# More rooms for the weight halves in the three double gate blocks of a fused decoder block

## The chip, the cores and the metric

The kernel runs on one core of one Trainium2 chip. The time is the device time of one execution in microseconds (us), taken as the median of the runs. The reader meets five engines and a queue: PE (TensorE, the matrix products), DVE (VectorE), ACT (ScalarE), POOL (GpSimd) and SP (SyncE), whose queue issues nearly all loads from memory. PEld is the part of PE that loads the stationary operand of a product.

## The reference

One layer of a decoder: 256 rows of 2048 numbers in float32. The input is normalised and modulated (shift, scale and gate come from a vector c through `w_ada`), and one wide projection `w_in` feeds three token mixers (stick-breaking attention, dilated attention, gated linear attention) and the gates of the three branches. What matters here are these lines:

```python
proj = h @ w_in
... gate_cols = the last 3 * 2048 columns of proj
g = jax.nn.sigmoid(gate_cols.reshape(b, t, N_BRANCH, d))
y = g[:, :, 0] * (o_sb @ w_br_sb) + g[:, :, 1] * (o_dil @ w_br_dil) + g[:, :, 2] * (o_gla @ w_br_gla)
x = x + gate1 * (y @ w_out)
```

After it comes a feed-forward part of the same kind (`w_ffn_in`, `w_ffn_out`). The gate columns are cut into four blocks of 512 columns for each of the three branches: twelve blocks of 2048 x 512 weights, times the 256 x 2048 matrix h.

## The kernel before

**Products.** Every float32 weight is split into two halves, hi (the weight rounded to the matrix engine's format) and lo (the rest), and each product is three matrix instructions: hi by hi, lo by hi, hi by lo (`mm3`, L173 to L175). The columns of h are the stationary operand, 128 x 512 weights the moving one, and the results add up in PSUM banks of 128 x 512.

**A weight tile's way.** A tile of 256 x 512 weights (512 KB) is loaded into a raw tile by SP (`raw_at`, L216), ACT copies it to the hi half (`split`, L236), DVE subtracts to give the lo half (`sub`, L222), and PE uses both. A place for a raw tile is called a raw here, a place for a pair of halves a room. The pool `wp` has four raws and four rooms; further ones are borrowed from named tiles of 128 x 1024 numbers or more that are out of use at the time, such as `T3`, `X1`, `X2`, `A9`, `A10`. `S(tag, ...)` takes the named tile; its new user waits until the last user of the old contents is done.

**Double blocks.** Of the twelve gate blocks, block 0 of each branch and block 3 of each are computed one by one (`gate_block`), and blocks 1 and 2 of a branch together (`gate_pair`, one call for each branch: 0, 1 and 2). `gate_pair` goes through eight steps, n = 0 to 7, in the order of `GATE_PAIRS`. Six steps are plain: two weight tiles (c0 and c1, one of each block), two rooms, 24 matrix instructions. Two of them (n = 2 and n = 5) are fast: two weight tiles r0 and r1 are combined by four more DVE subtractions, with `A0` and `A1` as places for the sums, to seven products instead of eight (Strassen's way), so that four rooms and 21 matrix instructions do. After the second fast step, the shared products are added to the results by `fast_products` (copy L315, sums L316 to L319, adds to the banks L273), the first two adds between steps 6 and 7, the others after step 7. A sigmoid (ACT, L1208) then writes the gates to `A7`/`X0` (branch 0), `A8`/`X1` (branch 1) and `T0`/`X2` (branch 2).

**Which raw and which room.** Both are taken in turn. With e extra rooms, room number i of a cycle of 4 + e is extra room i if i < e, else the next room of the pool. `gate_pair` sets the count so that each call begins with the four rooms of the pool. A call uses 20 rooms, numbered k = 0 to 19: k = 0, 1 in step 0; 2, 3 in step 1; 4 to 7 in step 2 (fast); 8 to 11 in steps 3 and 4; 12 to 15 in step 5 (fast); 16, 17 in step 6; 18, 19 in step 7. The raws, 16 in a call and numbered j = 0 to 15 (two in each step), go by a count that runs on from one call to the next.

**Order.** The weights of three steps are asked for ahead (`LOOK` = 3), with a raised priority (`prio`); the merging sums have twice that. The order of instructions on each engine is laid out beforehand by a planner, which takes the instruction of the highest priority that is ready by its own estimate of times; on the chip each engine keeps that order, and so does the SP queue with its loads. Between the splits lie the background sums for the modulation (`ada_mac`, L424), which read tiles of `w_ada` (L520) from a small ring; in the three double blocks they make the sum for gate1 in `T4` and `T5`. `ada` is the accumulator of the other background sums, 128 x 2048 numbers wide.

Of the kernel before, what the change touches and what calls it, by code (L numbers as in the profile page):

```python
# [11 lines left out]
F32R = mybir.dt.float32r  # L12
# [5 lines left out]
P = 128  # L18
# [5 lines left out]
NB = 512  # L24
# [56 lines left out]
def trunk(ctx: ExitStack, tc: tile.TileContext, I, out):  # L81
# [12 lines left out]
    def nm(base):  # L94
        uid[0] += 1
        return f"{base}_{uid[0]}"

    def S(tag, shape, dtype=F32):
        return slot.tile(shape, dtype, tag=tag, name=nm(tag))
# [13 lines left out]
    @contextmanager  # L113
    def prio(offset=AHEAD):

        with tc.high_priority(offset=offset):
            start = tc.cur_priority
            yield
            n = tc.cur_priority - start
        tc.cur_priority += n  # L120
# [80 lines left out]
    def sums_of(sf, h, a, b):  # L201

        (a0, b0), (a1, b1) = ((x[:, a, :], x[:, b, :]) for x in h)
        for dst, x, y, op in (
            (0, a1, b1, ALU.add), (2, a0, a1, ALU.subtract), (1, sf[:, 0], a0, ALU.subtract), (3, b0, sf[:, 1], ALU.subtract)
        ):
            nc.vector.tensor_tensor(sf[:, dst], x, y, op=op)

    def load_pair(src, p, c0, c1, fast, tags):


        def raw_at(c):
            more_raws = state.get("more_raws", ())
            i = state["raws"] = (state.get("raws", -1) + 1) % (4 + len(more_raws))
            raw = S(more_raws[i], [P, 2, NB]) if i < len(more_raws) else wp.tile([P, 2, NB], F32, tag="raw", name=nm("raw"))
            nc.sync.dma_start(raw, src[2 * p * P : (2 * p + 2) * P, c : c + NB].rearrange("(k p) c -> p k c", p=P))  # L216
            return raw

        def sub(dst, x, y):
            chain = state.get("chain")  # L220
            with tc.issue_after(chain.ins) if chain is not None else nullcontext():
                done = nc.vector.tensor_tensor(dst, x, y, op=ALU.subtract)  # L222
            if "chain" in state:
                state["chain"] = done
            return done

        def split(src):
            n = src.shape[1]
            more_rooms = state.get("more_rooms", ())
            i = state["tiles"] = (state.get("tiles", -1) + 1) % (4 + len(more_rooms))  # L230
            if i < len(more_rooms):
                hi, lo = (S(tag, [P, 2, NB], F32R) for tag in more_rooms[i])
            else:
                hi = wp.tile([P, 2, NB], F32R, tag="whi", name=nm("whi"), bufs=4)
                lo = wp.tile([P, 2, NB], F32R, tag="wlo", name=nm("wlo"), bufs=4)
            nc.scalar.copy(hi[:, :n, :], src)  # L236
            state["split"] = sub(lo[:, :n, :], src, hi[:, :n, :].bitcast(F32))
            return [(hi[:, i, :], lo[:, i, :]) for i in range(n)]

        with prio():  # L240
            if not fast:
                return [split(raw_at(c0)), split(raw_at(c1))]
            r0, r1 = raw_at(c0), raw_at(c1)
            b11, b21 = split(r0)
            ta, tb = (S(tag, [P, 2, NB]) for tag in tags)
            sub(ta[:, 0], r1[:, 0], r0[:, 0])
            sub(ta[:, 1], r1[:, 1], r1[:, 0])
            (b22,) = split(r1[:, 1:2])
            sub(tb[:, 0], r1[:, 1], ta[:, 0])
            sub(tb[:, 1], r0[:, 1], tb[:, 0])  # L250
            t1, t3 = split(ta)
            t2, t4 = split(tb)
            return b11, b21, b22, t1, t3, t2, t4

    def fast_products(src, c0, c1, order, at, sums, own, other, tags, hooks={}, more=False, look=None):
# [4 lines left out]
        def load(n):  # L260
            while len(ws) < min(n, len(order)):
                ws.append(load_pair(src, order[len(ws)][0], c0, c1, order[len(ws)][1], tags))
                splits.append(state["split"])
# [935 lines left out]
    def gate_pair(br, own, other, rooms, raws=()):  # L1199
        state["more_rooms"], state["more_raws"] = rooms, raws  # L1200
        state["tiles"] = len(rooms) - 1
        c0 = COL_G + br * D + NB
        o = fast_products(w_in, c0, c0 + NB, GATE_PAIRS, h_at, h_sums, own, other, ("A0", "A1"), look=LOOK)
        with prio():
            for i in range(2):
                g = S(gtags[1 + i][br], [P, NT, NB])
                for t in range(NT):
                    nc.scalar.activation(g[:, t, :], o[i][t], AF.Sigmoid)  # L1208
                gates[1 + i, br] = g
# [38 lines left out]
    for j in range(2):  # L1248
        hi = S(gtag[0][j], [P, 4, T], F32R)
        lo = S(gtag[1][j], [P, 4, T], F32R)  # L1250
# [64 lines left out]
    h_sums = sums_of_h()  # L1315
    state["rate"] = RATE_PAIRS
    ring["tags"], ring["spare"] = ("AR0", "AR1", "KD"), 1
    gate_pair(0, acc_bank, misc_bank, (("X1", "X2"), ("A9", "A10")), ("T3",))
    gate_pair(1, misc_bank, acc_bank, (("A9", "A10"),), ("X2", "T3"))
    gate_pair(2, acc_bank, misc_bank, (("A9", "A10"),), ("T3",))  # L1320
    ring["tags"] = ("AR0", "AR1", "KC", "KD")
    ring["spare"] = 2
    state["rate"] = RATE_Y
# [164 lines left out]
    for i in range(NFF):  # L1488
# [30 lines left out]
        if ftags[2 * i] == ftags[2 * i + 1]:  # L1519
            hl = S(ftags[2 * i], [P, 2, 4, T], F32R)  # L1520
            hi, lo = hl[:, 0], hl[:, 1]
        else:
            hi, lo = (S(tag, [P, 4, T], F32R) for tag in ftags[2 * i : 2 * i + 2])
# [140 lines left out]
```

## Time and profile before

| what | value |
|---|---|
| median of 3 runs (lowest to highest) | 1577.41 us (1577.26 to 1579.7) |
| the profiled execution | 1576.77 us, span 1575.0 us |
| PE busy | 1563.4 us, 99% of the span |
| DVE busy | 1394.3 us, 89% |
| ACT busy | 876.9 us, 56% |
| memory traffic | 255 GB/s over the span |

The span runs from the first to the last instruction of the profiled execution. A timeline row gives the start in us from the start of the span, the duration, the engine, the line, the operation, what it writes and reads (by tile names without numbers, so that `A` stands for any of A0 to A12, `X` for X0 to X2, `T` for T0 to T6), the shapes, and in square brackets the idle time before it with what ended that. The durations of matrix instructions overlap: the next one starts before the one before it ends, so the distance of two starts is what one costs. A row of waits gives the waiting instruction, what released it, the total in us, the number of times and the longest.

### The profile page before, as it was taken

The numbers are of one execution on the slowest core, as the hardware profiler recorded it, in microseconds if no ns is written. First come the engines' busy times: TensorE is split into PE (matmuls) and PEld (weight loads), VectorE is DVE, ScalarE is ACT, GpSimd is POOL, SyncE is SP. The second block draws the span as 40 slices with busy tenths as digits, with TensorE's granted clock in tenths as the row PEclk, the third lists the DMA queues.
The fourth block names the chain that finished last, engine by engine and source line by source line (L and its number), as shares of the span: only waits on it lengthen the run. The fifth ranks groups of instructions, "written<-read, shape, count | busy, mean of one in ns | idle before, by whom it ended". The sixth has DMA issues, their size and how long they took to land.

```text
span 1575.0 us, 20266 instructions
## 1 busy us (share of the span) xinstructions
PE 1563.4 (99%) x7186; PEld 1293.5 (82%) x7186; DVE 1394.3 (89%) x1704; ACT 876.9 (56%) x1215; POOL 12.6 (1%) x24
## 2 busy tenths in 40 slices
PE   8999999999999999999999999999999999999998
PEld 7878888888888788888888888888888888888887
DVE  6889996888888899987977888999999999899896
ACT  5654448875765545444435645556555555455553
POOL 1000000000000000000000000000000000000000
PEclk9999999999999999999999999999999999999999
DMA  9999997677787888989998886665666566876764
GB/s 333 361 326 323 336 308 239 221 237 224 240 293 256 269 290 273 316 255 320 305 329 258 299 301 205 188 212 188 201 203 211 174 201 231 291 229 202 222 212 136
DMA packets 196317, 402.26 MB, mean 255 GB/s; under 512 B 13102, under 2 KB 28116, under 8 KB 196216
## 3 DMA queue, kind: packets, MB, share of 16 engines
q1 hardware_dynamic: 194952, 397.75, 76.5%
q0 software_dynamic: 1088, 3.16, 0.5%
q8 instruction: 56, 0.92, 0.2%
q14 instruction: 45, 0.37, 0.1%
q10 hardware_dynamic: 176, 0.07, 0.0%
HBM read 395.68 MB, written 5.24 MB: 255 GB/s over the span
## 4 chain that ended last, share of the span: by engine, by line
PE 91%; DVE 4%; DMA 2%; ACT 2%; issue 1%; SPq 0%; DVEq 0%; ACTq 0%
PE acc L175 21%; PE acc L174 21%; PE acc L173 21%; PE misc L174 7%; PE misc L175 7%; PE misc L173 7%; DVE wlo L222 1%; PE acc L579 1%; PE misc L948 1%; DVE A L222 1%; PE misc L1287 1%; DVE T L424 0%; DVE wlo L166 0%; DMA A<-x 0%; PE misc L572 0%
## 5 line engine op out<-in xcount | busy, mean ns | idle before, releaser
L165 ACT CAST whi<-raw 128x1024 fp32r<-128x1024 f32 (+1 forms) x277 | 278.8, 1012 | 286.5 <-PE acc L175 193.1
L166 DVE TENSOR_TENSOR wlo<-raw,whi 128x1024 fp32r<-128x1024 f32 (+1 forms) x277 | 322.0, 1171 | 93.8 <-ACT whi L165 92.5
L173 PE MATMUL acc<-whi,H 128*128 128x512 f32 x997 | 390.5, 392 | 1.2 <-ACT H L591 0.8
L174 PE MATMUL acc<-wlo,H 128*128 128x512 f32 x997 | 388.9, 390 | 0.8 <-DVE wlo L166 0.7
L175 PE MATMUL acc<-whi,H 128*128 128x512 f32 x997 | 388.8, 391 | 0.5 <-DVE H L598 0.4
L175 PEld LDWEIGHTS acc<-whi,H 128*128 128x128 f32 x997 | 187.0, 188 | 40.2 <-DVE H L598 1.4
L173 PEld LDWEIGHTS acc<-whi,H 128*128 128x128 f32 x997 | 187.2, 188 | 39.9 <-ACT H L591 1.3
L174 PEld LDWEIGHTS acc<-wlo,H 128*128 128x128 f32 x997 | 187.4, 188 | 39.2 <-DVE wlo L166 1.7
L236 ACT CAST whi<-raw 128x1024 fp32r<-128x1024 f32 (+1 forms) x130 | 125.4, 975 | 66.0 <-PE acc L175 32.7
L222 DVE TENSOR_TENSOR wlo<-raw,whi 128x1024 fp32r<-128x1024 f32 (+1 forms) x130 | 144.1, 1125 | 15.9 <-ACT whi L236 14.9
L175 PE MATMUL acc<-whi,A 128*128 128x512 f32 x221 | 86.1, 389 | 0.0
L173 PE MATMUL acc<-whi,A 128*128 128x512 f32 x210 | 82.0, 390 | 0.0
L174 PE MATMUL acc<-wlo,A 128*128 128x512 f32 x210 | 81.7, 389 | 0.0
L174 PE MATMUL misc<-wlo,H 128*128 128x512 f32 (+1 forms) x190 | 73.6, 387 | 1.3 <-DVE wlo L222 1.3
L173 PE MATMUL misc<-whi,H 128*128 128x512 f32 (+1 forms) x190 | 73.6, 387 | 0.0
L175 PE MATMUL misc<-whi,H 128*128 128x512 f32 (+1 forms) x190 | 73.5, 387 | 0.0
L222 DVE TENSOR_TENSOR A<-raw,A 128x1024 fp32r<-128x1024 f32 (+2 forms) x54 | 53.8, 1002 | 1.3 <-ACT A L236 0.8
L424 DVE SCALAR_TENSOR_TENSOR ada<-AR,csil,ada 128x1024 f32<-128x1024 f32 x39 | 49.7, 1279 | 5.1 <-DMA AR<-w_ada 5.0
L175 PEld LDWEIGHTS acc<-whi,A 128*128 128x128 f32 x221 | 41.5, 188 | 8.7
L236 ACT CAST A<-raw 128x1024 fp32r<-128x1024 f32 (+1 forms) x36 | 35.9, 1003 | 21.7 <-PE acc L175 7.2
L174 PEld LDWEIGHTS acc<-wlo,A 128*128 128x128 f32 x210 | 39.4, 188 | 8.1
L173 PEld LDWEIGHTS acc<-whi,A 128*128 128x128 f32 x210 | 39.4, 188 | 8.0
(682 smaller groups left out, 3038.3 us busy)
## 6 DMA issues: line engine op xcount, KB each, us to landing
raw<-w_in SPq DMA_DIRECT2D x192, 512.0 KB, 4.7
raw<-w_ffn_in SPq DMA_DIRECT2D x135, 512.0 KB, 4.7
raw<-w_ffn_out SPq DMA_DIRECT2D x73, 512.0 KB, 4.7
AR<-w_ada SPq DMA_DIRECT2D x62, 512.0 KB, 4.9
raw<-w_out SPq DMA_DIRECT2D x32, 512.0 KB, 5.6
OS<-w_ada SPq DMA_DIRECT2D x24, 512.0 KB, 6.1
KD<-w_ada SPq DMA_DIRECT2D x22, 512.0 KB, 5.5
AR<-w_ffn_in SPq DMA_DIRECT2D x22, 512.0 KB, 4.2
```

The lines of the kernel that those rows point to most:

```text
L165: state["cast"] = nc.scalar.copy(hi[:, :n, :], raw[:, :n, :])
L166: state["split"] = nc.vector.tensor_tensor(lo[:, :n, :], raw[:, :n, :], hi[:, :n, :].bitcast(F32), op=ALU.subtract)
L173: nc.tensor.matmul(ps, lh, rh, start=start, stop=False, skip_group_check=seeded)
L174: nc.tensor.matmul(ps, lh, rl, start=False, stop=False, skip_group_check=seeded)
L175: state["mm"] = nc.tensor.matmul(ps, ll, rh, start=False, stop=stop, skip_group_check=seeded)
L222: done = nc.vector.tensor_tensor(dst, x, y, op=ALU.subtract)
L236: nc.scalar.copy(hi[:, :n, :], src)
L424: nc.vector.scalar_tensor_tensor(acc, raw, c, acc, op0=ALU.mult, op1=ALU.add)
L579: state["warm"] = nc.tensor.matmul(ps, ones_r, wide, start=True, stop=True)
L948: nc.tensor.matmul(ps[:n, t * N_GLA + h, :].rearrange("p (s l) -> p s l", l=L), at(f, h, t)[:, :n], odd(at(f, h, t)), start=True, stop=True,)
L1287: nc.tensor.transpose(ps[:, i, :], src[:, i * P : (i + 1) * P], ident)
```

## The change

The extra rooms and raws of the three calls are extended by named tiles. A room may now be one tile that holds both halves (`ada`). No load, no product and no sum is added or removed.

```diff
+    def room(tags):
+        if len(tags) == 1:
+            hl = S(tags[0], [P, 2, 2, NB], F32R)
+            return hl[:, 0], hl[:, 1]
+        return (S(tag, [P, 2, NB], F32R) for tag in tags)
...
             if i < len(more_rooms):
-                hi, lo = (S(tag, [P, 2, NB], F32R) for tag in more_rooms[i])
+                hi, lo = room(more_rooms[i])
...
-    gate_pair(0, acc_bank, misc_bank, (("X1", "X2"), ("A9", "A10")), ("T3",))
-    gate_pair(1, misc_bank, acc_bank, (("A9", "A10"),), ("X2", "T3"))
-    gate_pair(2, acc_bank, misc_bank, (("A9", "A10"),), ("T3",))
+    gate_pair(0, acc_bank, misc_bank, (("X1", "X2"), ("A9", "A10"), ("ada",)), ("T3", "T0", "A8"))
+    gate_pair(1, misc_bank, acc_bank, (("A9", "A10"), ("X1", "T0"), ("ada",)), ("X2", "T3"))
+    gate_pair(2, acc_bank, misc_bank, (("A9", "A10"), ("ada",)), ("T3", "T0"))
```

| call | rooms before, after | raws before, after |
|---|---|---|
| branch 0 | 6, 7 | 5, 7 |
| branch 1 | 5, 7 | 6, 6 |
| branch 2 | 5, 6 | 5, 6 |

## The prediction

> **What bounds the kernel now.** I read the page first, then who waits for whom on PE, then the busy time in the stretches of the three double blocks, and there the timeline.
>
> ```profile
> span 1575.0 us, 20266 instructions
> ...
> PE 1563.4 (99%) x7186; PEld 1293.5 (82%) x7186; DVE 1394.3 (89%) x1704; ACT 876.9 (56%) x1215; POOL 12.6 (1%) x24
> ```
>
> PE is busy all the time but 11.6 us, so no change that leaves the products as they are can bring more than that, and this one only the share that lies in the double blocks. Who waits on PE (the longest, 2.5, is the start of the kernel):
>
> ```profile
> PE misc L351 <- DMA H<-c: 2.5, 1, 2.5
> ...
> PE misc L174 <- DVE wlo L222: 1.3, 1, 1.3
> ...
> PE acc L173 <- DVE acc L273: 0.3, 1, 0.3
> ```
>
> ```profile
> core 0: us, PE busy (x) PEld busy (x) DVE busy (x) ACT busy (x) POOL busy (x), PEclk, DMA share, GB/s
> ...
> 490.90:533.80 42.90, 42.55 (x189) 34.92 (x187) 40.26 (x49) 22.24 (x30) 0.00 (x0) 1.00 0.86 284
> 533.80:577.60 43.80, 42.52 (x187) 34.84 (x186) 40.87 (x45) 24.58 (x29) 0.00 (x0) 1.00 0.82 269
> 577.60:619.80 42.20, 42.20 (x188) 34.95 (x187) 40.47 (x44) 22.36 (x25) 0.00 (x0) 1.00 0.82 269
> ```
>
> These are the three calls. PE has two holes in them, one in branch 0 and one in branch 1; branch 2 has none. DVE is busy 93 to 96% of each. The two holes by their starts:
>
> ```profile
> 527.51 0.39 PE L175 MATMUL acc<-A,H 128*128 128x512 f32 x1
> 528.25 0.47 PE L173 MATMUL acc<-whi,H 128*128 128x512 f32 x1 [0.34 <-DVE acc L273]
> ...
> 549.25 0.39 PE L175 MATMUL misc<-whi,H 128*128 128x512 f32 x1
> 549.48 0.40 PE L173 MATMUL misc<-whi,H 128*128 128x512 f32 x1
> 551.16 0.50 PE L174 MATMUL misc<-wlo,H 128*128 128x512 f32 x1 [1.28 <-DVE wlo L222]
> ```
>
> A matrix instruction costs 0.227 (branch 2: 186 of them, 6 x 24 + 2 x 21, in 42.2 us). So the holes cost 528.25 - 527.51 - 0.23 = 0.51 and 551.16 - 549.48 - 0.23 = 1.45: 1.96 us is all there is to win here.
>
> **Hole one (1.45, branch 1, step 3).** The lo half that PE waits for:
>
> ```profile
> 541.10 0.68 DVE L222 TENSOR_TENSOR A<-X,A 128x512 f32<-128x512 f32 x1
> ...
> 546.25 0.69 DVE L222 TENSOR_TENSOR A<-X 128x512 f32<-128x512 f32 x1 [1.54 <-DMA X<-w_in]
> ...
> 549.89 1.22 DVE L222 TENSOR_TENSOR wlo<-T,whi 128x1024 fp32r<-128x1024 f32 x1
> ```
>
> ```profile
> 544.93 1.05 ACT L236 CAST whi<-T 128x1024 fp32r<-128x1024 f32 x1 [0.19 <-PE misc L175]
> ```
>
> ```profile
> 531.18 0.37 SPq L216 DMA_DIRECT2D T<-w_in  x1
> ```
>
> ```profile
> 533.80:577.60 43.80, 7.67 (x6) 1.00 0.82 269
> ```
>
> ACT had been waiting for PE, that is, for a free room, and started the copy 4.5 us ahead of the need. Step 3 uses rooms k = 8, 9. With five rooms, k = 8 takes the pool's room of k = 3, free when PE ends step 1. With seven, it takes that of k = 1, free when PE ends step 0, 24 x 0.227 = 5.4 us sooner. The tile `T` was there (load issued at 531.18), so copy and split can come some 5 us earlier; DVE finds the time because the background sums (last row: six in this call, 7.67) have no product waiting. The hole goes: -1.45. If DVE kept its old order the gain would be 0; more than the hole cannot be won.
>
> **Hole two (0.51, branch 0, before step 7).** PE waits for the merging adds, which DVE reached late:
>
> ```profile
> 523.29 1.22 DVE L222 TENSOR_TENSOR wlo<-T,whi 128x1024 fp32r<-128x1024 f32 x1
> 524.42 0.68 DVE L316 TENSOR_TENSOR KC<-misc,T 128x512 f32<-128x512 f32 x1
> ...
> 527.41 0.69 DVE L273 TENSOR_TENSOR acc<-acc,T 128x512 f32<-128x512 f32 x1
> ```
>
> Three splits of steps 6 and 7 stood in front of L316. The rooms k = 17 and 18 now hang on the ends of k = 10 and 11 instead of k = 11 and 12; k = 17 comes free 12 products = 2.7 us sooner, k = 18 six (1.4). Splits that are done 1.4 to 2.7 us earlier leave L316 free to start as much earlier, and 0.51 is enough: -0.51. Between the ends 0 (order kept, or the next call's splits pushed in front) and -0.51 I take the latter.
>
> The long wait beside it is off PE's path:
>
> ```profile
> 520.17 1.05 ACT L236 CAST whi<-T 128x1024 fp32r<-128x1024 f32 x1
> 528.85 1.05 ACT L236 CAST whi<-T 128x1024 fp32r<-128x1024 f32 x1 [7.63 <-DMA T<-w_in]
> ```
>
> In before, `T3` is the raw of j = 15 of branch 0 and of j = 0 of branch 1, so a load waits for the split of the one just before it. After, the cycle of seven ends branch 0 on `T3`, `T0` (j = 14, 15) and branch 1 begins on four pool raws; `X2` and `T3` fall on j = 4, 5 and 10, 11, the raws of its two fast steps. This wait goes; PE was fed all the same, so it counts 0.
>
> **The new wait (branch 2, step 0).** In branch 1 the cycle of seven rooms puts k = 19 on `X1`/`T0`, with lo in `T0`: it is read by the last 12 products of the call. In branch 2, `T0` is the raw of j = 1, the tile of c1 in step 0. Its load cannot go out before PE's last reading of `T0`, and step 0 needs it 12 products after. In before, the same place:
>
> ```profile
> 577.15 0.39 PE L174 MATMUL misc<-A,H 128*128 128x512 f32 x1
> 577.38 0.39 PE L175 MATMUL misc<-A,H 128*128 128x512 f32 x1
> 577.61 0.39 PE L173 MATMUL acc<-whi,H 128*128 128x512 f32 x1
> ```
>
> Take 577.61, branch 2's first product, as zero. `T0` is free at 577.15 + 0.39 = -0.07. A load that waited for its tile shows the rest:
>
> ```profile
> 541.86 0.37 SPq L216 DMA_DIRECT2D X<-w_in  x1
> ```
>
> `X` was last read until 541.78, the load was issued 0.08 later, and DVE's waiting subtraction began at 546.25, 4.4 after the issue. So: issue 0.0, landed 4.4, hi ready 4.4 + 1.05 = 5.5, lo ready (split 1.22, two hand-overs of 0.05) 6.8. PE's own: 12 products of c0 until 2.7. If PE does them as written, it waits from 2.7 to 5.5, does one product, and waits to 6.8: 6.8 - 2.7 - 0.23 = 3.8 us. But the planner orders PE by readiness:
>
> ```profile
> 442.90 0.61 PE L1076 MATMUL misc<-ident,T 128*128 128x128 f32 x3
> 443.26 0.48 PE L173 MATMUL acc<-whi,H 128*128 128x512 f32 x1
> 443.58 0.40 PE L174 MATMUL acc<-wlo,H 128*128 128x512 f32 x1
> 443.82 0.30 PE L1076 MATMUL misc<-ident,T 128*128 128x128 f32 x1
> ```
>
> Nine transposes written in one piece were broken up with products there, as their data came. At step 0 it can pull the 12 products of c0 of step 1 ahead (other banks, no fast step, weights in a pool raw); those of c1 cannot go, since c1 of step 0 opens their banks. All 12 ahead leaves 6.8 - 5.4 - 0.23 = 1.1. The planner counts on loads too early: it put `A<-X` where it idled 1.54. If it expects `T0` 1.5 sooner, it pulls only six (6 x 0.227 = 1.4, to 4.1) ahead of the first hi product, which then waits from 4.1 to 5.5: 1.4, and the other six cover the split. Bounds 0 (parts of the fast step 2 pulled too) and +3.8; I take +1.4, since the `X` row is a load of this very kind.
>
> In the Trainium skill, "DMA: Bandwidth & Descriptors", section "Anatomy of one DMA", a transfer costs about 2.0 us plus its bytes over 436 GB/s; for 512 KB that is an estimated 3.2 us, 1.2 less than the `X` row, and by it the new wait would be some 0.2 to 2.6. The trace disagrees here (4.4; the page's median for these loads is below), so its number stands.
>
> ```profile
> raw<-w_in SPq DMA_DIRECT2D x192, 512.0 KB, 4.7
> ```
>
> **The other tiles.** The last readers of `ada` and of the attention's tiles, and the next sum in `ada`:
>
> ```profile
> L474 PE MATMUL misc<-ident,ada x16: 270/272/275, 462.8 to 478.2; 128*128 128x128 f32 x16
> ```
>
> ```profile
> L1086 PE MATMUL misc<-scr,A x12: 377/379/382, 448.3 to 456.9; 128*128 128x256 f32 x12
> ```
>
> ```profile
> L424 DVE SCALAR_TENSOR_TENSOR ada<-KD,csil,ada x8: 1277/1278/1280, 644.8 to 771.7; 128x1024 f32<-128x1024 f32 x8
> ```
>
> `ada` is free from 478.5 to 644.8, and each use as a room lies between: 0. `T0` and `A8` are free as raws for branch 0 from 457: 0; at worst one load (512 KB at 269 GB/s, 1.9 us) gets ahead of the block in progress. `X1`/`X2` in branch 1: `X2` is free 2.7 before branch 0's end, lands 1.8 after it, and step 2 needs its first half at 10.9 and its last at 15.0; three splits of 1.22 and five half-size ones of 0.69 are 7.1, so 0. `T0` later in branch 2 (j = 7, 13): three steps of lead, 0. SP stands still behind the `T0` load only if that is placed before its time; behind it are tiles for steps 3 on, 16 us away.
>
> Sum: -1.45 - 0.51 + 1.4 = -0.6 us. On the profiled execution 1576.77 gives 1576.2; the median of the three runs is 0.64 above it, so on 1577.41 I predict 1576.9.
>
> **The rivals.** *All covered:* step 2's products fill too, the new wait is 0, both holes go: 1577.41 - 1.96 = 1575.4. For it: ACT and DVE have time in branch 2. Against: the load alone lasts 4.4.
>
> *As written (slower):* the planner leaves c1 of step 0 in its place: +3.8 - 1.96 = +1.8, or +2.4 with hole two kept: 1579.2 to 1579.8. It is slower than before once the new wait is over 1.96, and by more than 0.2% once it is over 5.1. For it: at 549.48 PE stood in front of a lo half with nothing pulled ahead. Against: there nothing else was ready.
>
> *Holes stay:* DVE is nearly full, and the rooms only move its queue; holes as before, and the new wait of 1.4 to 3.8 on top: 1578.8 to 1581.2. For it: 93 to 96% busy. Against: six background sums a call can give way.
>
> *Half clock:* the products after a long hole run slowly, as the first of the kernel do:
>
> ```profile
> 2.67 3.78 PE L579 MATMUL acc<-H,ones_r 128*128 128x512 f32 x8
> ```
>
> Eight at 0.47 instead of 0.227 cost 1.9 more: with the wait of 3.8 as written 1581.1 to 1581.7. The Trainium skill, "TensorE: Matmul & The Clock Gate", section "Part 1: The HAM clock gate", says that an idle window of about 3.4 us halves the clock. The trace tells only that a hole of 1.45 left the granted clock at 1.00 (stretch 533.80 to 577.60). The waits here come in two parts, 2.8 and 1.0, so I give it little.
>
> **How the numbers follow.** 0.2% of 1577 is 3.2 us, about what a measurement here tells from no change. Forecast (within 1575.9 to 1578.5) 0.45; all covered 0.2; as written 0.16; holes stay 0.11; half clock or something unseen in the planner's new order 0.08. Faster by 0.2% would need more than the holes: 0.03, out of the last case. Slower by 0.2% (over 1580.6): half of "holes stay", the rest of the last case, and the tail of "as written": 0.17. The rest, 0.8, is within. Range 1575.2 to 1580.8; the forecast's own is 1575.9 to 1578.5.
>
> **What would show it.** No PE idle at branch 1's step 3 and before branch 0's step 7; a load `T<-w_in` issued right at the end of branch 1, its copy 4.4 us later, and there PE waiting for ACT L236 or DVE L222; ACT's 7.6 us wait gone; PE's busy time unchanged. Wrong if the new wait is over 2.5 us, or if a hole opens in a fast step, where X and T are reloaded late.

## The result and the profile after

The changed kernel takes 1582.7 us (median of 8 runs, 1581.0 to 1583.9) against 1576.9 of the kernel before, run beside it (8 runs, 1575.5 to 1579.7): a ratio of 1.0034 with an interval of 1.0025 to 1.0043. It is slower by a third of a percent, and 1.9 us above the range of the prediction. The profiled execution took 1583.55 us, its span is 6.8 longer than that of before. In the new file every line behind the function `room` stands 7 further down (L216, L222, L236, L273, L424 are now L223, L229, L243, L280, L431).

The page of after:

```profile
span 1581.8 us, 20267 instructions
...
PE 1566.6 (99%) x7186; PEld 1295.5 (82%) x7186; DVE 1393.9 (88%) x1704; ACT 877.6 (55%) x1215; POOL 12.7 (1%) x24
```

The work is the same, but PE's busy time has grown by 3.2: some of its products last longer. Who waits on PE, in after (total, times, longest):

```profile
PE acc L173 <- ACT whi L243: 3.7, 1, 3.7
...
PE misc L877 <- ACT A L802: 1.2, 1, 1.2
...
PE misc L173 <- DVE A L1270: 0.5, 1, 0.5
PE misc L173 <- DVE misc L280: 0.2, 1, 0.2
```

The two waits of before are gone, four others stand there. Three of them lie in the double blocks, and here is the timeline of PE around them:

```profile
511.26 0.39 PE L173 MATMUL acc<-whi,H 128*128 128x512 f32 x1
512.15 0.47 PE L173 MATMUL misc<-whi,T 128*128 128x512 f32 x1 [0.50 <-DVE A L1270]
...
571.66 0.39 PE L175 MATMUL misc<-whi,H 128*128 128x512 f32 x1
572.20 0.47 PE L173 MATMUL misc<-A,H 128*128 128x512 f32 x1 [0.15 <-DVE misc L280]
...
577.76 0.39 PE L173 MATMUL acc<-whi,H 128*128 128x512 f32 x1
...
580.49 0.39 PE L173 MATMUL misc<-A,H 128*128 128x512 f32 x1
...
580.94 0.39 PE L175 MATMUL misc<-A,H 128*128 128x512 f32 x1
585.05 2.17 PE L173 MATMUL acc<-whi,H 128*128 128x512 f32 x4 [3.73 <-ACT whi L243]
...
590.43 0.63 PE L174 MATMUL acc<-wlo,H 128*128 128x512 f32 x1
590.86 0.45 PE L175 MATMUL acc<-whi,H 128*128 128x512 f32 x1
591.15 0.39 PE L174 MATMUL acc<-wlo,H 128*128 128x512 f32 x1
```

A hole is again the distance of two starts less 0.227. In branch 0's fast step 2 there is one of 512.15 - 511.26 - 0.23 = 0.66; before branch 1's step 7 one of 0.31; and in branch 2's step 0, which starts at 577.76, one of 585.05 - 580.94 - 0.23 = 3.9. Behind it the products come every 0.43 (590.43 to 590.86) instead of every 0.227: 14 distances from 585.05 to 591.15 are 6.10, where 14 x 0.227 would be 3.18, so 2.9 more is lost there (0.26 of it in two longer distances at the head, 0.59 and 0.52). The granted clock (the number behind the busy times of the five engines; here the rows from the end of the hole to behind the slow stretch) says why:

```profile
583.10:584.10 1.00, 0.00 (x0) 0.00 (x0) 0.00 (x0) 0.14 (x1) 0.00 (x0) 1.00 0.09 31
584.20:585.00 0.80, 0.00 (x0) 0.00 (x0) 0.00 (x0) 0.80 (x2) 0.00 (x0) 0.50 0.00 0
585.10:591.00 5.90, 5.90 (x14) 4.39 (x15) 5.76 (x5) 2.75 (x3) 0.00 (x0) 0.50 0.59 174
591.00:595.00 4.00, 4.00 (x19) 3.29 (x18) 2.57 (x3) 2.11 (x2) 0.00 (x0) 1.00 0.74 274
```

The clock is halved between 584.1 and 584.2, while PE still waits: it had been idle for 3.0 then, since 580.94 + 0.23 = 581.17.

So the account is 3.9 + 2.9 + 0.66 + 0.31 = 7.8 of new loss, less 1.96 of old: +5.8 in the double blocks. The other 1.0 of the span lies outside them: branch 0's first product starts at 492.09, in before at 490.89. The wait in L877 above, some 300 us before the hole in a part that the change does not touch, accounts for it (1.2 here; it was 0.5 in the first and 0.7 in the fifth of the experiments below, and is not among the longest of before).

Why was the third hole 3.9? The queue of SP, ACT and DVE at that place:

```profile
560.35 0.38 SPq L223 DMA_DIRECT2D raw<-w_in  x1
...
565.51 2.21 SPq L223 DMA_DIRECT2D raw<-w_in  x3
...
576.60 2.79 SPq L223 DMA_DIRECT2D raw<-w_in  x2
579.48 7.17 SPq L223 DMA_DIRECT2D T<-w_in  x2
```

```profile
583.96 1.04 ACT L243 CAST whi<-T 128x1024 fp32r<-128x1024 f32 x1 [3.72 <-DMA T<-w_in]
584.91 1.99 ACT L243 CAST whi<-raw 128x1024 fp32r<-128x1024 f32 x2
```

```profile
577.78 1.21 DVE L229 TENSOR_TENSOR A<-raw,A 128x1024 fp32r<-128x1024 f32 x1
578.91 0.69 DVE L280 TENSOR_TENSOR misc<-misc,KC 128x512 f32<-128x512 f32 x1
585.03 1.23 DVE L229 TENSOR_TENSOR wlo<-T,whi 128x1024 fp32r<-128x1024 f32 x1 [5.43 <-ACT whi L243]
```

Two things are to be seen. The load of `T0` went out at 579.48, 1.7 after branch 2's first product, though `T0` was free by then. In SP's queue two loads into pool raws stood in front of it. The first went out at 576.60, the second only at 579.02 (its row ends at 579.39 and one such load takes 0.37), since DVE was reading the raw that it needed until 577.78 + 1.21 = 578.99. And on ACT the copy of `T0` stands in front of the two copies of step 1 (`whi<-raw`, 584.91). By the turn of the raws, the tiles of step 1 are the first two of the four pool loads above (560.35 and 565.51), asked for long before. But the rooms are handed out in turn too, and the room of `T0`'s tile comes first. That this turn is what holds step 1 back is read from ACT's order here; two of the runs below bear it out. PE had nothing of step 1 to pull ahead; the three products at 580.49 to 580.94 are of the fast step 2.

### The profile page after: what moved, and what is told of

Its sections match the earlier page's. It is cut to its first block, busy times and chain, and to the rows that moved or that the text cites. A ratio compares the mean times of both kernels' runs of the same rounds, so it can differ in the third digit from the quotient of the medians.

```text
span 1581.8 us, 20267 instructions
## 1 busy us (share of the span) xinstructions
PE 1566.6 (99%) x7186; PEld 1295.5 (82%) x7186; DVE 1393.9 (88%) x1704; ACT 877.6 (55%) x1215; POOL 12.7 (1%) x24
## 4 chain that ended last, share of the span: by engine, by line
PE 89%; DVE 4%; ACT 3%; DMA 2%; issue 1%; SPq 0%; ACTq 0%; DVEq 0%
PE acc L175 21%; PE acc L173 21%; PE acc L174 21%; PE misc L173 7%; PE misc L175 7%; PE misc L174 7%; DMA raw<-w_in 1%; DVE A L229 1%; PE acc L586 1%; PE misc L955 1%; ACT whi L165 1%; PE misc L1294 1%; DMA X<-w_in 1%; DVE wlo L166 0%; DMA A<-x 0%
## 5 line engine op out<-in xcount | busy, mean ns | idle before, releaser
L173 PE MATMUL acc<-whi,H 128*128 128x512 f32 (+1 forms) x994 | 390.5, 394 | 4.6 <-ACT whi L243 3.7
L174 PE MATMUL acc<-wlo,H 128*128 128x512 f32 (+1 forms) x994 | 388.7, 391 | 0.8 <-DVE wlo L166 0.7
L175 PE MATMUL acc<-whi,H 128*128 128x512 f32 (+1 forms) x994 | 388.5, 392 | 0.5 <-DVE H L605 0.4
L243 ACT CAST whi<-raw 128x1024 fp32r<-128x1024 f32 (+1 forms) x130 | 124.0, 966 | 76.4 <-PE acc L175 38.3
L229 DVE TENSOR_TENSOR wlo<-raw,whi 128x1024 fp32r<-128x1024 f32 (+1 forms) x130 | 143.3, 1114 | 11.7 <-ACT whi L243 10.6
L173 PE MATMUL misc<-whi,H 128*128 128x512 f32 (+1 forms) x223 | 86.8, 389 | 0.0
L175 PE MATMUL misc<-whi,H 128*128 128x512 f32 (+1 forms) x223 | 86.4, 388 | 0.0
L174 PE MATMUL misc<-wlo,H 128*128 128x512 f32 (+1 forms) x223 | 86.3, 387 | 0.0
L175 PE MATMUL acc<-whi,A 128*128 128x512 f32 x210 | 81.8, 389 | 0.0
L173 PE MATMUL acc<-whi,A 128*128 128x512 f32 x206 | 80.5, 391 | 0.0
L431 DVE SCALAR_TENSOR_TENSOR ada<-AR,csil,ada 128x1024 f32<-128x1024 f32 x39 | 49.7, 1280 | 4.5 <-DMA AR<-w_ada 4.5
L175 PEld LDWEIGHTS misc<-whi,H 128*128 128x128 f32 x223 | 41.9, 188 | 8.7
L174 PEld LDWEIGHTS misc<-wlo,H 128*128 128x128 f32 x223 | 41.9, 188 | 8.4
L173 PEld LDWEIGHTS misc<-whi,H 128*128 128x128 f32 x223 | 41.9, 188 | 8.4
L175 PEld LDWEIGHTS acc<-whi,A 128*128 128x128 f32 x210 | 39.4, 188 | 8.3
L229 DVE TENSOR_TENSOR A<-raw,A 128x1024 fp32r<-128x1024 f32 (+2 forms) x48 | 44.7, 933 | 0.8 <-ACT A L243 0.4
```

The lines of the kernel that those rows point to most:

```text
L173: nc.tensor.matmul(ps, lh, rh, start=start, stop=False, skip_group_check=seeded)
L174: nc.tensor.matmul(ps, lh, rl, start=False, stop=False, skip_group_check=seeded)
L175: state["mm"] = nc.tensor.matmul(ps, ll, rh, start=False, stop=stop, skip_group_check=seeded)
L431: nc.vector.scalar_tensor_tensor(acc, raw, c, acc, op0=ALU.mult, op1=ALU.add)
```

## The experiments

Each stands beside its own runs of the kernel before, whose medians were 1577.12 (the first four), 1576.36 (the next four) and 1576.63 (the last four). They are edits of the changed kernel, except where a part of the change is put alone into the kernel before. "Hole" is the distance of two starts less 0.227.

**Is `T0` as a raw of branch 2 the price?** It is taken out of branch 2's raws:

```diff
-    gate_pair(2, ..., (("A9", "A10"), ("ada",)), ("T3", "T0"))
+    gate_pair(2, ..., (("A9", "A10"), ("ada",)), ("T3",))
```

> The changed kernel with one raw less in branch 2 (T3 alone, as in the kernel before); rooms and raws of branches 0 and 1 stay. Theory: the whole loss is the chain T0's last reading - its load - its halves, a hole of 3.9 us on PE with a stretch of slow products behind it (about 2.9 us). Without it both go: 1582.7 - 6.8 = 1575.9 us, 1.0 below the kernel before, and the two holes of before (0.51 and 1.45) stay away. Rival, that the larger number of rooms shifts DVE's queue and the loss is spread: still above 1580 us.

Measured: 1577.59, ratio 1.0005 (0.9996 to 1.0014). Branch 2 has no hole any more and no slow stretch. But the gain that was to remain is not there: the double blocks have one hole of 1.54, at 571.88 before branch 1's step 7, where before had none.

```profile
570.11 0.39 PE L175 MATMUL misc<-whi,H 128*128 128x512 f32 x1
571.88 0.47 PE L173 MATMUL misc<-A,H 128*128 128x512 f32 x1 [1.38 <-DVE misc L280]
```

**The same room, free sooner.** `X1`/`T0` is made the first of branch 1's extra rooms, so that it serves k = 18 instead of k = 19 and is free 12 products (2.7) earlier:

```diff
-    gate_pair(1, ..., (("A9", "A10"), ("X1", "T0"), ("ada",)), ("X2", "T3"))
+    gate_pair(1, ..., (("X1", "T0"), ("A9", "A10"), ("ada",)), ("X2", "T3"))
```

> The changed kernel with the extra rooms of branch 1 in another order (X1/T0 first, then A9/A10, then ada), so that T0 is read for the last time 12 products (2.7 us) before the end of branch 1 and not at its end. Theory: the hole shrinks by 2.7 us to about 1.2, which is too short to slow the clock, so the slow stretch goes as a whole: 1582.7 - 2.7 - 2.9 = 1577.1 us. Rival, the slow stretch has another cause than the hole: 1582.7 - 2.7 = 1580.0 us.

Measured: 1578.7, ratio 1.0007 (0.9998 to 1.0016). The hole is 1.28 (580.74 - 579.23 - 0.23), and the clock stays whole behind it:

```profile
577.50:583.00 5.50, 4.38 (x19) 3.15 (x18) 3.80 (x4) 5.50 (x8) 0.00 (x0) 1.00 0.49 150
```

The hole is 2.6 shorter and the tile is free 2.7 sooner, as expected, but that the two agree is luck:

```profile
573.99 0.37 SPq L223 DMA_DIRECT2D T<-w_in  x1
```

```profile
579.63 1.06 ACT L243 CAST whi<-T 128x1024 fp32r<-128x1024 f32 x1
```

The load of `T0` went out 2.75 before branch 2's first product (576.74), where in after it was 1.7 behind it: 4.5 sooner. ACT's copy follows 5.6 after the load and no longer waits for it: two sigmoids, a copy of step 2 and a third sigmoid fill ACT from 577.24 on, and step 1's copies stand behind `T0`'s again (580.57). What is left of the hole here comes from ACT's order. The median lies 1.6 above the 1577.1 that was expected; the trace does not show why.

**Another turn of the rooms.** In branch 2 the count begins with the extra rooms, so that `T0`'s tile and the first tile of step 1 no longer stand behind each other in the pool:

```diff
-    gate_pair(2, ..., (("A9", "A10"), ("ada",)), ("T3", "T0"))
+    gate_pair(2, ..., (("ada",), ("A9", "A10")), ("T3", "T0"))
...
-        state["tiles"] = len(rooms) - 1
+        state["tiles"] = -1 if br == 2 else len(rooms) - 1
```

> The changed kernel; in branch 2 the cycle of rooms begins with its extra rooms, ada for the first tile and A9/A10 for the tile in T0, and the four pool rooms follow. The load of T0 is as late as before. Theory: products of step 1 could not be pulled ahead because the pool gives its rooms in turn and step 1's rooms stood behind the one of the late tile; with a room of its own for that tile, ten to twelve products of step 1 fill 2.3 to 2.7 us of the hole, the rest (about 1.5) is too short for the slow stretch: 1582.7 - 2.4 - 2.9 = 1577.4 us. Rival, step 1 is held back by something else (its banks, its load): 1582.7 us as before.

Measured: 1576.9, ratio 0.9998 (0.9989 to 1.0006). `T0` serves the same places in both calls as in after, and the hole is 0.64:

```profile
577.00 0.39 PE L173 MATMUL acc<-ada,H 128*128 128x512 f32 x1
...
579.72 0.39 PE L173 MATMUL acc<-whi,H 128*128 128x512 f32 x1
...
581.75 0.39 PE L173 MATMUL acc<-whi,H 128*128 128x512 f32 x1
582.62 0.73 PE L173 MATMUL acc<-A,H 128*128 128x512 f32 x2 [0.47 <-ACT A L243]
```

```profile
576.96 0.37 SPq L223 DMA_DIRECT2D T<-w_in  x1
```

Both causes seen in after are gone together. The load goes out at 576.96, at the start of the branch (1.8 sooner than in after, by that start), and PE pulls ten products of step 1 ahead (579.72 to 581.75) where after had three of step 2 (seven more, 1.6). 1.8 + 1.6 = 3.4 is about what the hole lost (3.9 - 0.64 = 3.3). ACT copies step 1's raws at 564.58 and 571.59 here and `T0`'s tile behind them, at 581.52; in after they came behind `T0`'s, at 584.91. A hole of 0.68 stands before branch 1's step 7, so that the time is again that of the kernel before.

**Is the slow stretch the clock's answer to the hole?** Sixteen products into a bank that is not in use are put behind the first 12 products of branch 2, to keep PE busy while it waits; they change no result:

```diff
+                    if (n, c) == (0, 0) and state.get("fill"):
+                        dummy = other([P, NB])
+                        moving = hT[0][0][:, 0:2, :].rearrange("p a b -> p (a b)")
+                        for _ in range(state.pop("fill")):
+                            with tc.issue_after(state["mm"].ins):
+                                state["mm"] = nc.tensor.matmul(dummy, hT[0][0][:, 0, :P], moving, start=True, stop=True)
```

> The changed kernel with 16 more products of 128x512 (of tiles of h with themselves, into a bank that is not read) on PE right behind the first 12 products of branch 2, where the hole is; they use 3.6 us. Theory: T0's halves come when they came, so the products go on at the same time as before, but PE was never idle for long and the products behind the hole run at 0.227 us instead of 0.427: 2.9 us less, 1579.8 us, or 1580.5 if the three products of step 2 that stood in the hole now come after it. Rival, the slow products have another cause than the idle time: 1582.7 us or more.

Measured: 1581.69, ratio 1.0028 (1.0018 to 1.0039).

```profile
580.57 3.79 PE L324 MATMUL misc<-H 128*128 128x512 f32 x16
585.90 0.73 PE L173 MATMUL acc<-whi,H 128*128 128x512 f32 x2 [1.54 <-ACT whi L243]
...
587.42 0.39 PE L174 MATMUL acc<-wlo,H 128*128 128x512 f32 x1
587.65 0.40 PE L175 MATMUL acc<-whi,H 128*128 128x512 f32 x1
```

Behind the filled hole the products come every 0.23 at once, and the granted clock is 1.00 from 580 to 590: the slow stretch belongs to the idle time. Idle pieces of 1.70 (before 585.90) and 0.38 are left. The whole time gained little, since the edit cost as much elsewhere: relative to branch 2's start the load of `T0` goes out 0.7 later than in after, the three products of step 2 (0.68) no longer fall into the hole, and the holes of branch 0's step 2 and before branch 1's step 7 are 0.96 and 0.78, 0.3 and 0.5 more.

**`T0` out of the last step of branch 1.** The room `X1`/`T0` becomes the last extra room, which is used last at k = 13:

```diff
+    gate_pair(1, ..., (("A9", "A10"), ("ada",), ("X1", "T0")), ("X2", "T3"))
```

> The changed kernel with the extra rooms of branch 1 in the order A9/A10, ada, X1/T0, so that T0 is read for the last time in the fast step 5, two plain steps before the end of branch 1; all rooms and raws of the change are used. Theory: no wait for T0 is left, no slow stretch, and what stays is a wait for the merging adds before step 7 of branch 1 as in the run without the raw in T0 (1.54 us there): 1577.5 us, no change against before. Rival, that wait came with the order of that one run: 1576.0 us.

Measured: 1576.42, ratio 1.0005 (0.9995 to 1.0014). No hole in branch 2, though `T0` is a raw there; one of 1.43 is left before branch 1's step 7 (the profile puts this one down to a copy on ACT). With the first experiment: neither the room in branch 1's last step nor the raw alone costs anything in branch 2, only the pair of both does.

**`T0` one tile earlier.** The raws of branch 2 in the other order, so that `T0` takes the other of the first two tiles' places:

```diff
+    gate_pair(2, ..., (("A9", "A10"), ("ada",)), ("T0", "T3"))
```

> The changed kernel with the two extra raws of branch 2 in the other order: the late tile T0 now carries the first weights of step 0 (c0), T3 the second (c1). Theory, the pool's rooms are given in turn: neither c1 of step 0 nor step 1 can be split before T0 has landed, so the 12 products that ran before the hole are missing too: the hole grows by 2.7 us to 6.6, with the same slow stretch: 1582.7 + 2.7 = 1585.4 us. Rival, the tiles that have landed go first: the hole stays as it is, 1582.7 us.

Measured: 1585.94, ratio 1.0059 (1.0047 to 1.0072).

```profile
578.92 0.50 PE L174 MATMUL misc<-A,H 128*128 128x512 f32 x1 [1.84 <-DVE A L229]
579.25 0.40 PE L175 MATMUL misc<-A,H 128*128 128x512 f32 x1
584.96 1.22 PE L173 MATMUL acc<-whi,H 128*128 128x512 f32 x2 [5.31 <-ACT whi L243]
```

With the late tile in front of everything in the turn, the branch's own first products wait: 5.5, after one of 2.0, and a slow stretch again. The tile of c1, in `T3`, had been asked for at 553.27, and still ACT copies it only behind `T0`'s (both from 583.86 on), and step 1's two behind that (585.76): the turn holds back tiles that are there.

**Branch 0's part alone.** Branches 1 and 2 are as before:

```diff
-    gate_pair(0, ..., (("X1", "X2"), ("A9", "A10")), ("T3",))
+    gate_pair(0, ..., (("X1", "X2"), ("A9", "A10"), ("ada",)), ("T3", "T0", "A8"))
```

> The kernel before with the change of branch 0 alone (seven rooms and seven raws there). The prediction's step for hole two: 0.5 us less, so 1576.6 us, and hole one stays, since branch 1 has its five rooms. Rival, the rooms bring splits in front of the combining sums of a fast step in branch 0 (a wait of 0.67 us stands there in the changed kernel): 1577.1 to 1577.8 us.

Measured: 1575.54, ratio 0.9994 (0.9985 to 1.0003). Hole two is gone, and so is hole one, which lies in branch 1, where nothing was changed. A hole of 0.68 in branch 0's step 2 is new.

**Branch 1's part alone.** The other way round:

```diff
-    gate_pair(1, ..., (("A9", "A10"),), ("X2", "T3"))
+    gate_pair(1, ..., (("A9", "A10"), ("X1", "T0"), ("ada",)), ("X2", "T3"))
```

> The kernel before with the change of branch 1 alone (seven rooms there; branches 0 and 2 as before, so T0 is no raw). The prediction's step for hole one: the wait of 1.45 us in step 3 goes and nothing takes its place: 1577.1 - 1.45 = 1575.7 us. Rival: splits and background sums that come earlier stand in front of the merging sums, and a wait before step 7 of branch 1 takes the place of the one in step 3: 1577.1 us.

Measured: 1577.12, ratio 1.0006 (0.9997 to 1.0015). Hole one is gone, and of hole two 0.16 is left, though branch 0 is as before. But PE waits 2.5 before step 7 of branch 1, and eight products soon after it are slow (574.43 to 577.79, 3.36 where 8 x 0.227 would be 1.82); the profiled execution, of 1579.29, is one of the longer ones:

```profile
570.25 0.39 PE L175 MATMUL misc<-whi,H 128*128 128x512 f32 x1
572.96 0.47 PE L173 MATMUL misc<-A,H 128*128 128x512 f32 x1 [2.32 <-DVE misc L280]
...
574.43 0.58 PE L173 MATMUL misc<-A,H 128*128 128x512 f32 x1
574.81 0.63 PE L174 MATMUL misc<-A,H 128*128 128x512 f32 x1
575.23 0.63 PE L175 MATMUL misc<-A,H 128*128 128x512 f32 x1
```

```profile
572.90:574.40 1.50, 1.44 (x6) 1.24 (x7) 1.50 (x3) 1.25 (x2) 0.00 (x0) 1.00 1.06 392
574.40:577.40 3.00, 3.00 (x9) 2.32 (x8) 3.00 (x4) 0.87 (x3) 0.00 (x0) 0.51 0.83 280
```

What made the merging sums late? DVE's background sums (L431) in the 19 us ahead of step 7, first in this run, then in that of branch 0's part alone:

```profile
553.00:572.00 19.00, 7.59 (x6) 1.00 0.86 292
```

```profile
553.00:572.00 19.00, 3.83 (x3) 1.00 0.91 309
```

Six against three. The merging sums begin at 569.20 in the one and at 566.07 in the other; three sums of 1.28 are 3.8.

**Fewer background sums.** The run above with the background sums at half their rate during branch 1 (the rest of them comes later):

```diff
+    state["rate"] = RATE_PAIRS / 2
     gate_pair(1, ..., (("A9", "A10"), ("X1", "T0"), ("ada",)), ("X2", "T3"))
+    state["rate"] = RATE_PAIRS
```

> As the run with the change of branch 1 alone, but with background sums handed out at half the rate during branch 1 (the others come later). That run had a hole of 2.3 us before step 7 of branch 1, with six background sums of 1.28 us on DVE in the 13 us before the merging sums, against three where branch 1 has five rooms. Theory: the rooms end the splits sooner, so the background sums bound to them come sooner too and stand in front of the merging sums; with half of them away the hole goes: 1.5 to 2 us less than the kernel before. Rival, DVE's order of splits alone makes the merging sums late: a hole of over 1 us stays there and the time is that of the kernel before.

Measured: 1576.2, ratio 0.9999 (0.9990 to 1.0008). Three sums in that stretch instead of six, the merging sums begin at 566.40, and the hole before step 7 is gone; hole two, in branch 0, is left with 0.55. In the trace the double blocks take 127.3 (491.83 to 619.10) where before had 128.9 (490.89 to 619.77), 1.6 less, as expected. The expected gain in the time is not there: outside the double blocks this execution is 1.1 longer, and the medians do not differ.

**Branch 0: raws or rooms?** First the raws of branch 0 alone, then its extra room alone, all else as before:

```diff
+    gate_pair(0, ..., (("X1", "X2"), ("A9", "A10")), ("T3", "T0", "A8"))
```

> The kernel before with the raws of branch 0 alone extended (T3, T0, A8), rooms as before. With rooms and raws of branch 0 extended both holes were gone (0.8 us less in the median). Theory: the raws did it, since T3 no longer carries two tiles in a row: ACT's wait of 7.6 us and DVE's idle moments behind it go, and DVE is ahead in branch 1: the hole of 1.45 us in step 3 of branch 1 goes, 1.0 to 1.5 us less than the kernel before. Rival, the rooms did it: both holes stay, no change.

```diff
+    gate_pair(0, ..., (("X1", "X2"), ("A9", "A10"), ("ada",)), ("T3",))
```

> The kernel before with the rooms of branch 0 alone extended (ada as a third), raws as before. Theory (the raws did it): ACT's wait for T3 stays and with it the hole in step 3 of branch 1; no change against before. Rival (the rooms did it): 1.0 to 1.5 us less.

Measured: with the raws 1576.47, ratio 0.9997 (0.9988 to 1.0006); with the room 1574.75, ratio 0.9989 (0.9980 to 0.9997). The raws remove holes one and two and bring a new one of 1.18 in branch 0's step 2. The room leaves 0.32 of each hole and brings none. In the run with the room, ACT still waits for `T3` as long as before:

```profile
ACT whi L243 <- DMA T<-w_in: 10.9, 2, 8.2
```

So most of the gain can be had without touching that wait. With the raws the wait is gone and both holes with it, so that it did no harm can't be said from these runs; either part alone is enough. What the raws cost is to be seen on DVE, where the sum that PE waits for (L1263 before, L1270 after) stands in before, and then in the run with the raws:

```profile
503.67 0.47 DVE L1263 SCALAR_TENSOR_TENSOR A<-misc,vec,A 128x256 fp32r<-128x256 f32 x1
```

```profile
509.92 0.48 DVE L1270 SCALAR_TENSOR_TENSOR A<-misc,vec,A 128x256 fp32r<-128x256 f32 x1
```

With the raws, six splits and subtractions of the later steps' tiles come ahead of it, from 504.17 to 509.92. This is read from the two orders; no run put the sum back alone.

**Without branch 1's part.** Branches 0 and 2 changed, branch 1 as before:

```diff
-    gate_pair(1, ..., (("A9", "A10"), ("X1", "T0"), ("ada",)), ("X2", "T3"))
+    gate_pair(1, ..., (("A9", "A10"),), ("X2", "T3"))
```

> The changed kernel with branch 1 as in the kernel before: branches 0 and 2 have all their new rooms and raws, T0 as a raw of branch 2 among them, but T0 is no room of branch 1. Theory: T0 does harm only as a room of the last step of one call and a raw of the first step of the next; here it is free long before, there is no hole at the start of branch 2 and both holes of before are gone through branch 0: 1.0 to 1.9 us less than the kernel before, the fastest of the set. Rival, the new raws of branch 2 cost something by themselves: slower than with branch 0 alone, 0 to 2 us over the kernel before.

Measured: 1575.23, ratio 0.9989 (0.9980 to 0.9998), span 1572.5; the double blocks take 127.0 (490.47 to 617.51), 1.8 less than in before. The only wait on PE left in the three calls (a hole of 0.35):

```profile
PE misc L173 <- DVE A L1270: 0.2, 1, 0.2
```

This version is faster than both kernels, by 0.1% against before. Branch 2's raw `T0` costs nothing once branch 1 no longer ends in it.

## Why the prediction was wrong

**The new wait: the step that failed.** Its place, its tile and its waiting instruction were right, its size was not: 3.9 instead of 1.4, just above the upper bound of 3.8. The landing was right (4.4 said; 583.96 - 579.48 = 4.5). Two parts of its working failed. "Issue 0.0" was 1.7: the step took the tile's freedom for the issue, though the load stood in one queue behind a load that waited for DVE. The prediction had asked only whether `T0`'s load would hold up those behind it. And "weights in a pool raw" was taken to mean that step 1 could be pulled ahead: the raws were there, but the rooms come in turn, and their turn was behind `T0`'s. So three products came ahead where the step took six, 0.7 less. The issue's 1.7, this 0.7 and the landing's 0.1 are the 2.5 between 1.4 and 3.9. With another turn of the rooms, which changed both parts, 0.64 is left. The section "Anatomy of one DMA" of the Trainium skill's "DMA: Bandwidth & Descriptors", which the prediction compares with its 4.4, is on transfers that GpSimd issues. These loads are SP's, so that 4.4 and 4.5 neither bear it out nor speak against it.

**Half clock: a rival that came true at 0.08.** It was given little because the wait was to come in two parts; it came in one. A slow product costs 0.43 where 0.47 was said, but 14 of them were slow and not eight: 2.9. The filled hole shows that the idle time is the cause. The Trainium skill, "TensorE: Matmul & The Clock Gate", section "Part 1: The HAM clock gate", has an idle window of about 3.4 us before the clock is halved. The traces do not bear this out as idle time in one piece: in after the clock was halved 3.0 into the hole, in the run with `T0` first 2.8 into the hole of 5.5 (between 582.2 and 582.3, idle since 579.48, though a hole of 2.0 stands just before it), and with branch 1's part alone 1.5 after a hole of only 2.5. In the profiled executions, holes up to 1.70 left the products as they were. No run fixes a limit.

**Hole one: right about its place, wrong about the sum.** PE no longer waits in branch 1's step 3, as said. But with two more rooms in that branch the same work was late at another place of it: 2.5 before step 7 with branch 1's part alone, 1.54 and 1.43 in the first and fifth experiments, 0.31 in after and 0.38 to 0.78 in the second to fourth. The step had found the time for earlier splits in the background sums ("no product waiting"). They did not give way: six of them came ahead of the merging sums instead of three, and halving their rate closed the hole. The rival "holes stay" named this (the rooms only move DVE's queue), with the holes in their old places. And hole one needs no change in branch 1 at all: branch 0's raws alone remove it, and its extra room alone leaves 0.32 of it. The prediction did not look across the border of the calls. By which step the work of one call comes sooner in the next was not traced further.

**Hole two** went, -0.51 as said. The room that the step named takes 0.19 of it alone (0.32 is left), the raws alone take all. But it is not branch 0's part alone that moves it: with branch 1's part alone 0.16 is left, and 0.55 when the background sums are halved there; how a later call does that was not traced. Not foreseen in the sum was the hole of 0.66 in branch 0's fast step 2, of the kind that the prediction's last sentences name ("a hole opens in a fast step"), though not from a late load: it comes with branch 0's raws (1.18 with them alone, none with the room alone), as the splits that they bring forward stand ahead of a sum that PE needs.

**At nothing:** the run that keeps ACT's wait for `T3` has the lowest median of all (1574.75), so there was little to win by it, as said; 0 exactly is not shown. In after that wait is gone, but ACT idles 7.6 at another place, before a copy of branch 2's step 2 (573.97, for a raw's load). `ada` as a room cost nothing in branch 0, as said.

**The sign.** The sum of the measured terms is -1.96 for the old holes, +0.97 for the two small new ones, +3.9 for the wait and +2.9 for the clock: +5.8, where -0.6 was forecast. Of the 6.4 between them the clock makes 2.9, the mis-sized wait 2.5 and the two small holes 0.97. The rival on the slower side was priced for the wait alone (+1.8) and for the wait with eight slow products (up to +4.3); the chances for both together were too low, because the wait's lower values rested on products that the order of the rooms did not allow.

## What to carry to other kernels

When a borrowed buffer is used in two stages that follow each other, look at its last use in the first and its first use in the second; the price of a pair is not seen in either stage alone, and here taking out either one removed it. Where buffers are handed out in turn, a tile that comes late holds back those behind it, though their data is there: to say what can be pulled ahead, follow the turn, and the queue of the loads, and not only the tile. On a stage where DVE is nearly full, more room does not make time: ask which of its work comes sooner, and what that stands in front of.

## What the runs showed of the hardware

A hole on PE can cost nearly twice its length: 3.9 of idle time were followed by 14 slow products, and 5.5 by a slow stretch as well, while 1.28 and 1.54 cost only themselves. The slow stretch has its own length, not the hole's: the clock is halved from 584.1 to 591.0 in after and from 582.2 to 589.1 in the run with `T0` first, some 6.8 each, and from 574.4 to 577.9 behind the 2.5 hole, some 3.4, half as long. Only the part of it that falls on products costs time: of the 6.8, 0.9 lay in the 3.9 hole and 2.7 in the 5.5 hole, and 2.9 were lost behind the one and 2.2 behind the other (9 distances from 584.96 to 589.24 are 4.28, where 9 x 0.227 would be 2.04). After the 2.5 hole the slow products did not begin at once: six came at the full rate first.

Whether such a hole is always followed by a slow stretch is open. Of eleven times of the kernel with branch 1's part alone, the four longest (1579.1 to 1580.5) all have a mean granted clock of 0.999, and of the seven others (1575.8 to 1577.9) six have 1.000; but 0.999 also stands beside the fastest time of the kernel with branch 0's room alone (1574.44), so the mean does not settle it. The kernel before has 0.998 beside two of thirty times (1578.91 and 1579.82), though its profiled execution has no hole over 1.45 in the double blocks.
